# Row maxima on one core: 17 loads become 16, GpSimd's share grows from 36 to 53 squares, and most of its results return by small transfers

## The chip, the cores and the metric

The kernel runs on one core of a Trainium2 chip. The metric is the device time of one execution in microseconds (us). The time before is the median of three runs.

## What is computed

```python
def setup_inputs():
    batch, seq, dim = 32, 512, 1024
    return {"x": np.random.randn(batch, seq, dim).astype(np.float32)}

def reference(x):
    return np.max(x, axis=-1).astype(np.float32)
```

So 16384 rows of 1024 numbers come in (67.11 MB in float32), and one maximum for each row goes out (64 KB).

## The kernel before

**Units.** A *block* is 128 rows, one on each of the 128 partitions: 1024 numbers a partition, 0.524 MB. There are 128 blocks. A *square* is an eighth of a block, 128 rows by 128 columns.

**Loads.** `BLOCKS` lists how many blocks each load brings, in two groups; three blocks more, the last ones, come cut into six *pieces* (`PIECES`: which of the three blocks, and how many columns). All of it goes through one ring of 47 blocks in SBUF (`ring`), issued from SyncE's queue (loads L270, pieces L275). A load is issued as soon as the part of the ring that it fills has been read by all who need it. Transfers take eight semaphores in turn, and one that reuses a semaphore waits on its queue until the transfer that had it last has landed.

**VectorE's part.** `direct(j)` (d steps) reduces whole blocks of load j into the result columns, `partial(j)` (p steps) those squares of a shared block that GpSimd does not take, f steps the six pieces; all of it is the one reduction in `maximum`, L76. `merge` (m steps) joins the partial maxima of VectorE and GpSimd; m99 does it for the late loads together and is the last reduction of the kernel.

**GpSimd's part.** `SHARED` says for load j: of how many blocks (m) GpSimd takes how many squares each (parts), how many blocks go together in one chunk (per); the shared blocks are the load's last ones, and the fourth number is not used. Each chunk k runs through five steps:
- t (`turn`, L155): TensorE transposes each square into PSUM (`ps`), so that the 128 columns stand on the partitions.
- c (`fetch`, L166): ScalarE copies them to SBUF (`sb`, two buffers).
- r (`across`, L173): GpSimd's all-reduce takes the maximum over the partitions (`top`, two buffers); every partition then holds the row maxima, 128 for each square.
- b (`back`, L184): TensorE turns them back, one small matmul for each square, from partition 0 of `top` into `small` in PSUM.
- e (`keep`, L194): ScalarE copies them beside VectorE's partial maxima (`parts` or `joint`).

Before, chunks have two blocks of three squares or fewer, so at most 768 columns.

**Order.** `PLAN` is the order written out by hand; the number is the load for d, p and m, the chunk for t, c, r, b and e, and the piece for f. `in_turn` ties each instruction to the one before it on the same engine, so that the scheduler keeps the plan's order there. Loads and stores are not tied by it; they stand where the scheduler puts them.

**Stores.** Two stores go out from ScalarE's queue at the end: 116 columns (58 KB, L301), which wait for the first piece's reduction, and the last 12 columns (6 KB, L303), which wait for m99.

Of the kernel before, what the change touches and what calls it, by code (L numbers as in the profile page):

```python
# [8 lines left out]
F32 = mybir.dt.float32  # L9
# [1 line left out]


BLOCKS = [
    [2, 16, 14, 15, 13, 12, 10, 9, 8, 7, 6, 4],
    [3, 2, 2, 1, 1],
]
RING = 47

SHARED = {10: (6, 3, 2, 0), 12: (3, 3, 2, 0), 14: (2, 3, 1, 0), 16: (1, 3, 2, 0)}


RANK = {12: 1, 14: 2, 16: 2}


PIECES = [(2, 640), (0, 576), (1, 512), (1, 512), (0, 448), (2, 384)]


PLAN = """  # L30
    d0 d1 d2 d3 d4 d5 d6 d7 d8 d9 t0 p10 t1 c0 r0 t2 c1 d11 r1 c2 b0 e0 r2 b1 e1 t3 p12 t4
    c3 b2 c4 r3 d13 e2 r4 m10 t5 p14 b3 c5 t6 r5 d15 e3 b4 c6 t7 p16 e4 r6 b5 f0 c7 e5 f1 r7
    b6 f2 e6 f3 b7 f4 e7 f5 m99
""".split()

NOSYNC = mybir.DependencyInfo(mybir.DependencyClass.NoSync, mybir.DependencyReason.DATA)
# [4 lines left out]
def kernel(  # L41
# [5 lines left out]
    nc = tc.nc  # L47
    P = 128
    X = mybir.AxisListType.X
    ALU = mybir.AluOpType  # L50
# [7 lines left out]
    once = ctx.enter_context(tc.tile_pool(name="once", bufs=1))  # L58
    turned = ctx.enter_context(tc.tile_pool(name="turned", bufs=2))
    allr = ctx.enter_context(tc.tile_pool(name="allr", bufs=2))  # L60
    psum = ctx.enter_context(tc.tile_pool(name="psum", bufs=2, space=bass.MemoryType.PSUM))
    psmall = ctx.enter_context(tc.tile_pool(name="psmall", bufs=4, space=bass.MemoryType.PSUM))

# [5 lines left out]
    def in_turn(engine, inst):  # L69
        if engine in latest:  # L70
            tc.add_manual_dep(inst.ins, latest[engine].ins.name, NOSYNC, reason="in turn")
        latest[engine] = inst
        return inst

    def maximum(out, in_):
        return in_turn("DVE", nc.vector.reduce_max(out=out, in_=in_, axis=X))  # L76

    ident = once.tile([P, P], F32)
# [5 lines left out]
        out=colno, data0=ident, data1=ident, initial=-1.0, op0=ALU.add, op1=ALU.mult))  # L84
    in_turn("DVE", nc.vector.transpose(out=rowno, in_=colno[:, :32]))  # L85
    for q in range(1, P // 32):
        part = rowno[q * 32:(q + 1) * 32, 0:1]
        in_turn("DVE", nc.vector.tensor_scalar(  # L88
            out=part, in0=part, scalar1=float(q * 32), scalar2=None, op0=ALU.add))
    in_turn("DVE", nc.vector.tensor_scalar(  # L90
        out=ident, in0=colno, scalar1=rowno[:, 0:1], scalar2=None, op0=ALU.is_equal))

    loads = []
    views = []
    last = 1 + max(r for r, _ in PIECES)
    first = at = 0
    for sizes in BLOCKS:
# [5 lines left out]
        base = len(loads)  # L103
        b, place = 0, {}
        for i in sorted(range(len(sizes)), key=lambda i: RANK.get(base + i, 0)):
            place[i] = b
            b += sizes[i]
        for i, n in enumerate(sizes):
            if at + n > RING:
                at = 0  # L110
            b = place[i]
# [3 lines left out]
    assert first == I  # L115
    shared = [SHARED.get(j, (0, C, 1, 0)) for j in range(len(loads))]

    lead = [n - s[0] for (_, n, _, _), s in zip(loads, shared)]
    final = [j for j in range(len(loads)) if j in RANK]
    final.sort(key=lambda j: loads[j][3])  # L120
# [6 lines left out]
    chunks = []  # L127
# [3 lines left out]
    def rows(j):  # L131
        start, n, _, _ = loads[j]
        return ring[:, I + start * D:I + (start + n) * D].rearrange("p (i d) -> p i d", d=D)

    filled, turns, tops = {}, {}, {}
    fetched = {}
    smalls = {}

    def share(j):
        m, parts, _, _ = shared[j]  # L140
        if j in RANK:
            r = loads[j][3] + lead[j] - col0
            return joint[:, r:r + m, :]
        if j not in fetched:
            fetched[j] = once.tile([P, m, parts + (parts < C)], F32, name=f"parts{j}")
        return fetched[j]
# [30 lines left out]
    def back(k):  # L177
        j, r, q = chunks[k]
        parts = shared[j][1]
        small = psmall.tile([P, q, parts], F32)  # L180
        for i in range(q):
            for c in range(parts):
                w = (i * parts + c) * P
                in_turn("PE", nc.tensor.transpose(  # L184
                    out=small[:, i, c:c + 1],
                    in_=tops[k][0:1, w:w + P],
                    identity=ident[0:1, 0:1],
                ))

        smalls[k] = small  # L190

    def keep(k):
        j, r, q = chunks[k]
        in_turn("ACT", nc.scalar.copy(out=share(j)[:, r:r + q, :shared[j][1]], in_=smalls[k]))  # L194

    def select(k):
        j, _, q = chunks[k]
        B = q * shared[j][1]
        view = tops[k][:, :B * P].rearrange("p (b w) -> p b w", w=P)
        in_turn("POOL", nc.gpsimd.affine_select(  # L200
            out=view, in_=view, pattern=[[0, B], [-1, P]], compare_op=ALU.is_equal,
            fill=0.0, base=0, channel_multiplier=1))

    def sums(k):
        j, r, q = chunks[k]
        parts = shared[j][1]
        for i in range(q):
            for c in range(parts):
                w = (i * parts + c) * P
                in_turn("ACT", nc.scalar.activation(  # L210
                    out=tops[k][:, w:w + P], in_=tops[k][:, w:w + P],
                    func=mybir.ActivationFunctionType.Copy,
                    accum_out=share(j)[:, r + i, c:c + 1]))

    def direct(j):
        _, n, _, col = loads[j]
# [4 lines left out]
    def partial(j):  # L221
        m, parts = shared[j][:2]

        s = width - parts if j in RANK else 1
        maximum(share(j)[:, :, parts:], rows(j)[:, lead[j]:lead[j] + m, parts * P:].rearrange(
# [14 lines left out]
    before = [None] * last  # L240
    for r, w in PIECES:
        c, q = done[r], before[r]
# [33 lines left out]
            pieces.pop(0)  # L276

    gate = once.tile([P, 2], F32)
    steps = {"t": turn, "c": fetch, "r": across, "b": back, "e": keep, "s": select, "x": sums, "m": merge}
    for step in PLAN:  # L280
        issue()
        kind, k = step[0], int(step[1:])
# [50 lines left out]
```

## Time and profile before

| | us |
|---|---|
| median of three runs (163.75 to 163.92) | 163.78 |
| the profiled execution | 163.59 |
| its span, from the first to the last instruction | 161.81 |
| VectorE busy, 33 instructions | 135.5 (84%) |
| GpSimd busy, 13 instructions | 15.9 (10%) |
| TensorE matmul busy, 72 instructions | 13.3 (8%) |
| ScalarE busy, 17 instructions | 7.3 (5%) |
| input read, mean over the span | 67.11 MB, 415 GB/s |

Engines are named PE (TensorE), PEld (its weight loads), DVE (VectorE), ACT (ScalarE), POOL (GpSimd), SP (SyncE); a q behind the name means its queue, which issues transfers. L76 is line 76 of the kernel. The page divides the span into 40 slices of 4.05 us and gives the busy share in tenths. A timeline row is: start, duration, engine, line, operation, what it writes and reads, how many; in brackets the idle time of the engine before it and what ended that. A row on DMA issues gives KB and the time from issue to landing.

### The profile page before, as it was taken

To read this page: it belongs to the slowest core of one execution; us is meant where nothing else is said; L and a number is where in the kernel's file an instruction comes from. 1 tells how busy PE (TensorE), PEld (TensorE's weight loads), DVE (VectorE), ACT (ScalarE), POOL (GpSimd) and SP (SyncE) were. 2 spreads that over 40 slices of the span, in tenths; PEclk is the share of its full clock that TensorE was granted. 3 is DMA by queue.
4 is the path that set the end of the run, shared out by engine and by line. 5 is a ranking of instruction groups with operands and counts; after the bars stand their busy time and mean duration, and the time that the engine had idled before them with its cause. 6 is when DMAs were issued, how large, how long until landed. Compare 5 with 4: busy or idle time off the path is not lost.

```text
span 161.8 us, 304 instructions
## 1 busy us (share of the span) xinstructions
PE 13.3 (8%) x72; PEld 11.1 (7%) x72; DVE 135.5 (84%) x33; ACT 7.3 (5%) x17; POOL 15.9 (10%) x13
## 2 busy tenths in 40 slices
PE   0000000000000000000000000000000000647471
PEld 0000000000000000000000000000000000637350
DVE  3500009999999929999999999999999999999994
ACT  0020000000000000000000000000000000142230
POOL 0000000000000000000000000000000000097991
PEclk9999999999999999999999999999999999995555
DMA  5996998799999599999988997999999899999991
GB/s 198 579 486 292 518 472 383 312 454 454 486 486 486 243 454 421 421 448 561 401 389 389 486 466 344 437 437 421 478 429 439 376 475 395 433 410 412 408 389 38
DMA packets 3600, 67.18 MB, mean 415 GB/s; under 512 B 656, under 2 KB 912, under 8 KB 1680
## 3 DMA queue, kind: packets, MB, share of 16 engines
q1 hardware_dynamic: 3312, 67.11, 97.0%
q10 hardware_dynamic: 288, 0.07, 0.2%
HBM read 67.11 MB, written 0.07 MB: 415 GB/s over the span
## 4 chain that ended last, share of the span: by engine, by line
DVE 63%; DMA 35%; issue 0%; SPq 0%; DVEq 0%
DVE ring L76 58%; DMA ring<-in_x_dram 35%; DVE parts L76 3%; DVE joint L76 2%; SPq L270 0%; DVEq L328 0%; DVEq L76 0%
## 5 line engine op out<-in xcount | busy, mean ns | idle before, releaser
L76 DVE TENSOR_REDUCE ring<-ring 128x2 f32<-128x2048 f32 (+17 forms) x19 | 125.7, 6660 | 23.0 <-DMA ring<-in_x_dram 22.9
L173 POOL PARTITION_ALL_REDUCE top<-sb x8 | 15.6, 2013 | 134.9 <-ACT sb L166 134.5
L155 PE MATMUL ps<-ident,ring 128*128 128x128 f32 x36 | 8.9, 426 | 141.1 <-DMA ring<-in_x_dram 141.0
L155 PEld LDWEIGHTS ps<-ident,ring 128*128 128x128 f32 x36 | 7.0, 222 | 141.2 <-issue 141.2
L166 ACT COPY sb<-ps 128x768 f32<-128x768 f32 (+1 forms) x8 | 5.0, 640 | 139.1 <-PE ps L155 137.7
L184 PE MATMUL small<-ident,top 1*128 1x1 f32 x36 | 4.8, 238 | 4.4 <-POOL top L173 4.4
L184 PEld LDWEIGHTS small<-ident,top 1*128 1x128 f32 x36 | 4.1, 197 | 6.4 <-POOL top L173 5.0
L76 DVE TENSOR_REDUCE joint<-ring 128x3 f32<-128x1920 f32 (+2 forms) x3 | 4.4, 1483 | 0.0
L76 DVE TENSOR_REDUCE parts<-ring 128x6 f32<-128x3840 f32 x1 | 4.1, 4144 | 0.0
L166 ACT ACT_TABLE_LOAD x1 | 1.3, 1283 | 7.7 <-DVE ring L76 7.7
L194 ACT COPY joint<-small 128x3 f32<-128x3 f32 (+1 forms) x5 | 0.8, 164 | 2.3 <-PE small L184 2.3
L81 DVE MEMSET ident<- 128x128 f32 x1 | 0.2, 165 | 0.8 <-PEq L317 0.8
L288 POOL MEMSET gate<- 128x1 f32 x1 | 0.1, 100 | 7.3 <-DVE ring L76 7.3
L194 ACT COPY parts<-small 128x6 f32<-128x6 f32 x3 | 0.5, 166 | 2.6 <-PE small L184 2.5
L88 DVE TENSOR_SCALAR rowno<-rowno 32x1 f32<-32x1 f32 x3 | 0.4, 147 | 0.1
L83 DVE TENSOR_TENSOR_SCAN colno<-ident 128x128 f32<-128x128 f32 x1 | 0.4, 424 | 0.0
L90 DVE TENSOR_SCALAR ident<-colno,rowno 128x128 f32<-128x128 f32 x1 | 0.3, 286 | 0.0
L85 DVE STREAM_TRANSPOSE rowno<-colno 128x32 f32<-128x32 f32 x1 | 0.2, 211 | 0.0
L76 DVE TENSOR_REDUCE ring<-joint 128x6 f32<-128x24 f32 x1 | 0.2, 169 | 0.0
L76 DVE TENSOR_REDUCE ring<-parts 128x6 f32<-128x24 f32 x1 | 0.2, 168 | 0.0
L317 POOL MEMSET const-float32-0.0<- 128x1 f32 x1 | 0.1, 100 | 0.2 <-issue 0.2
L317 POOL MEMSET const-bfloat16-1.0<- 128x1 bf16 x1 | 0.1, 102 | 0.0
(3 smaller groups left out, 0.3 us busy)
## 6 DMA issues: line engine op xcount, KB each, us to landing
ring<-in_x_dram SPq DMA_DIRECT2D x1, 7680.0 KB, 57.6
ring<-in_x_dram SPq DMA_DIRECT2D x1, 7168.0 KB, 40.0
ring<-in_x_dram SPq DMA_DIRECT2D x1, 6656.0 KB, 33.6
ring<-in_x_dram SPq DMA_DIRECT2D x1, 6144.0 KB, 33.1
ring<-in_x_dram SPq DMA_DIRECT2D x1, 5120.0 KB, 26.2
ring<-in_x_dram SPq DMA_DIRECT2D x1, 4608.0 KB, 36.7
ring<-in_x_dram SPq DMA_DIRECT2D x1, 4096.0 KB, 32.9
ring<-in_x_dram SPq DMA_DIRECT2D x1, 3584.0 KB, 28.2
```

The lines of the kernel that those rows point to most:

```text
L76: return in_turn("DVE", nc.vector.reduce_max(out=out, in_=in_, axis=X))
L81: in_turn("DVE", nc.vector.memset(ident, 1.0))
L83: in_turn("DVE", nc.vector.tensor_tensor_scan(out=colno, data0=ident, data1=ident, initial=-1.0, op0=ALU.add, op1=ALU.mult))
L85: in_turn("DVE", nc.vector.transpose(out=rowno, in_=colno[:, :32]))
L88: in_turn("DVE", nc.vector.tensor_scalar(out=part, in0=part, scalar1=float(q * 32), scalar2=None, op0=ALU.add))
L90: in_turn("DVE", nc.vector.tensor_scalar(out=ident, in0=colno, scalar1=rowno[:, 0:1], scalar2=None, op0=ALU.is_equal))
L155: in_turn("PE", nc.tensor.transpose(out=ps[:, w:w + P], in_=rows(j)[:, lead[j] + r + i, c * P:(c + 1) * P], identity=ident,))
L166: in_turn("ACT", nc.scalar.copy(out=sb[:, :W], in_=filled[k][:, :W]))
L173: in_turn("POOL", nc.gpsimd.partition_all_reduce(top[:, :W], turns[k][:, :W], P, bass_isa.ReduceOp.max))
L184: in_turn("PE", nc.tensor.transpose(out=small[:, i, c:c + 1], in_=tops[k][0:1, w:w + P], identity=ident[0:1, 0:1],))
L194: in_turn("ACT", nc.scalar.copy(out=share(j)[:, r:r + q, :shared[j][1]], in_=smalls[k]))
L317: nc = _bacc.Bacc("TRN2", target_bir_lowering=False, num_devices=1)
```

## The change

Loads of 8 and 7 blocks go, and a second one of 15 comes in; the others keep their sizes. GpSimd now shares loads 8, 9, 10, 11, 13 and 15: all eight squares of two blocks of load 8 and of load 9 (one block a chunk, 1024 columns), one square of each of four blocks of load 10 (512 columns), and smaller chunks of three late loads (768, 384, 384, 384 and 256 columns). That makes ten chunks with 53 squares in place of eight with 36. Load 8 has 9 blocks, load 9 has 6.

For the first four chunks, 32 squares, a new step s (`spread`) comes between r and b: a transfer from ScalarE's queue takes the 1024 maxima from partition 0 of `top` to eight partitions of a new tile `lines` (two buffers), 128 on each, 4 KB in all; then `back` turns the eight squares in one matmul. The steps x and the old s, which the plan did not use, are deleted. The pieces keep their six sizes in another order, and the plan is new. The new transfer is not put through `in_turn`.

```diff
 BLOCKS = [
-    [2, 16, 14, 15, 13, 12, 10, 9, 8, 7, 6, 4],
+    [2, 16, 14, 15, 15, 13, 12, 10, 9, 6, 4],
     [3, 2, 2, 1, 1],
 ]
...
-SHARED = {10: (6, 3, 2, 0), 12: (3, 3, 2, 0), 14: (2, 3, 1, 0), 16: (1, 3, 2, 0)}
-RANK = {12: 1, 14: 2, 16: 2}
-PIECES = [(2, 640), (0, 576), (1, 512), (1, 512), (0, 448), (2, 384)]
+SHARED = {8: (2, 8, 1, 1), 9: (2, 8, 1, 1), 10: (4, 1, 8, 0), 11: (3, 3, 2, 0), 13: (2, 3, 1, 0), 15: (1, 2, 4, 0)}
+RANK = {11: 1, 13: 2, 15: 2}
+PIECES = [(0, 640), (1, 512), (2, 576), (1, 512), (2, 448), (0, 384)]
 PLAN = """
-    d0 d1 d2 d3 d4 d5 d6 d7 d8 d9 t0 p10 t1 c0 r0 t2 c1 d11 r1 c2 b0 e0 r2 b1 e1 t3 p12 t4
-    c3 b2 c4 r3 d13 e2 r4 m10 t5 p14 b3 c5 t6 r5 d15 e3 b4 c6 t7 p16 e4 r6 b5 f0 c7 e5 f1 r7
-    b6 f2 e6 f3 b7 f4 e7 f5 m99
+    d0 d1 d2 d3 d4 d5 d6 d7 t0 d8 t1 c0 r0 c1 r1 s0 t2 d9 b0 c2 t3 e0 r2 s1 c3 b1 t4 p10 e1
+    r3 s2 c4 b2 t5 e2 m8 p11 r4 s3 t6 c5 d12 b3 c6 b4 r5 e3 e4 m9 m10 p13 t7 t8 r6 c7 b5 d14
+    r7 e5 b6 c8 p15 t9 e6 f0 r8 c9 b7 f1 e7 f2 r9 b8 f3 e8 f4 b9 f5 e9 m99
 """.split()
...
+    spare = ctx.enter_context(tc.tile_pool(name="spare", bufs=2))
...
+    lines = {}
...
     def back(k):
         j, r, q = chunks[k]
         parts = shared[j][1]
         small = psmall.tile([P, q, parts], F32)
+        smalls[k] = small
+        if k in lines:
+            B = q * parts
+            in_turn("PE", nc.tensor.transpose(
+                out=small.rearrange("p i c -> p (i c)"), in_=lines[k][:B, :], identity=ident[:B, :B]))
+            return
...
+    def spread(k):
+        j, _, q = chunks[k]
+        B = q * shared[j][1]
+        lines[k] = spare.tile([P, P], F32, name="lines")
+        nc.scalar.dma_start(
+            out=lines[k][:B, :], in_=tops[k][0:1, :B * P].rearrange("o (b w) -> o b w", w=P))
...
-    steps = {"t": turn, "c": fetch, "r": across, "b": back, "e": keep, "s": select, "x": sums, "m": merge}
+    steps = {"t": turn, "c": fetch, "r": across, "b": back, "e": keep, "s": spread, "m": merge}
```

More of the change, by code (lines that the diff above doesn't have):

```diff
@@ L188, in back @@
                 ))
-        smalls[k] = small
     def keep(k):
@@ L194, in keep @@
         in_turn("ACT", nc.scalar.copy(out=share(j)[:, r:r + q, :shared[j][1]], in_=smalls[k]))
-    def select(k):
+    def spread(k):
         j, _, q = chunks[k]
         B = q * shared[j][1]
[L199 to L213, printed above, removed]
+        lines[k] = spare.tile([P, P], F32, name="lines")
+        nc.scalar.dma_start(
+            out=lines[k][:B, :], in_=tops[k][0:1, :B * P].rearrange("o (b w) -> o b w", w=P))
     def direct(j):
```

## The prediction

> **What bounds the kernel now.** I read the page's strips of 40 slices first, then busy time by stretches, then the timeline of the last 25 us engine by engine, with the DMA issues for when transfers landed. The profiled execution took 163.59 us: a span of 161.81 and 1.78 around it. It lies 0.19 under the median of 163.78; I sum against the profiled one and add the difference to the median.
>
> ```profile
> DVE 3500009999999929999999999999999999999994
> ...
> POOL 0000000000000000000000000000000000097991
> ...
> DMA  5996998799999599999988997999999899999991
> ```
>
> VectorE and the DMA are both full from slice 15 on; GpSimd works only at the end. Which one leads?
>
> ```profile
> 60.00:90.00 30.00, 0.00 (x0) 0.00 (x0) 29.84 (x2) 0.00 (x0) 0.00 (x0) 1.00 1.00 430
> 90.00:120.00 30.00, 0.00 (x0) 0.00 (x0) 29.97 (x3) 0.00 (x0) 0.00 (x0) 1.00 1.00 433
> 120.00:140.00 20.00, 1.19 (x6) 1.22 (x7) 20.00 (x4) 0.00 (x0) 0.00 (x0) 1.00 0.98 419
> ```
>
> The stretches show the two last columns, DMA share and GB/s: 430 to 433 GB/s at a share of 1.00, whatever VectorE does. The input is one stream that never pauses; its last piece was issued at 153.44 and took 5.3 us, so it landed at 158.7. VectorE ran level with it:
>
> ```profile
> 155.56 3.86 DVE L76 TENSOR_REDUCE ring<-ring 128x1 f32<-128x640 f32 x6
> 159.33 0.17 DVE L76 TENSOR_REDUCE ring<-joint 128x6 f32<-128x24 f32 x1
> ```
>
> Six pieces, each taken about when it lands; the last (0.54 us from 158.87) starts 0.15 after its landing. So work taken off VectorE shortens nothing beyond that 0.15; less work for it is hidden by the stream. What does have slack is GpSimd's path:
>
> ```profile
> 141.25 7.48 POOL L173 PARTITION_ALL_REDUCE top<-sb  x3 [133.47 <-ACT sb L166]
> 149.75 3.91 POOL L173 PARTITION_ALL_REDUCE top<-sb  x2 [1.02 <-ACT sb L166]
> 154.05 4.24 POOL L173 PARTITION_ALL_REDUCE top<-sb  x3 [0.39 <-PE small L184]
> ```
>
> The last result ends at 158.29; three transposes and ScalarE's copy follow, and the copy ends at 159.02:
>
> ```profile
> 158.85 0.16 ACT L194 COPY joint<-small 128x3 f32<-128x3 f32 x1 [1.25 <-PE small L184]
> 158.92 0.38 ACTq L301 DMA_DIRECT2D out_dram<-ring  x1
> 159.53 0.34 ACTq L303 DMA_DIRECT2D out_dram<-ring  x1
> ```
>
> The final merge (m99) started at 159.33, so this path had 0.3 us to spare. That is the number the change must not overrun.
>
> **One load fewer.** Same bytes, and 15 blocks stand where 8 and 7 stood. The 15-block load occupied the stream from 41.6 to 59.7 (18.1 us; issue plus time to landing), the 8 and 7 together from 113.0 to 131.2 (18.2). Gain: 0.07 us on every later landing. The pieces keep their sizes, and VectorE takes them in the new order: 0 for the stream, and for VectorE the same six durations. The ring keeps up: the 10-block load is issued when VectorE ends the second 15 blocks, at about 94, with the 13 in hand landed at 93.6 and the 12 streaming until 108.1. The 9-block load ends at block 106, where the 7-block load ended before, at 131.2; the 6-block load is where it was, 138.5.
>
> **VectorE** is relieved of 17 squares (about 0.13 us each, 2.3 us) and gets two merges more (0.09 each in step). All of that is hidden by the stream, except 0.07 to 0.15 us at the end.
>
> **GpSimd.** Three 768-wide reductions take 7.48 us (2.49 each), three 384-wide ones 4.24 (1.41 each). A line through the two: 0.33 + 2.81 ns a column, so 1024 wide is 3.21, 512 1.77, 256 1.05. It is an estimate; the bounds are 2.49 (no dearer than 768) and 3.32 (in proportion to it). I take the line, as 1024 is nearest to 768 and fixed cost is small. The new list is 4 x 3.21 + 1.77 + 2.49 + 3 x 1.41 + 1.05 = 22.4 us in place of 15.6. It starts earlier: t0 now reads the 9-block load. From the 6-block landing at 138.57 to the first copy took 1.79 us with six transposes; two more at 0.21 give 2.2, so c0 runs 133.4 to 134.4 (768 wide took 0.80, 384 0.48: 1024 is 1.01) and r0 starts at 134.45. Without a gap GpSimd would end at 156.9, well in time.
>
> **The gaps.** The built program's order decides here. Copies and reductions are held in the plan's order, but the new small transfers are not tied into it: on ScalarE's queue s1 stands directly behind s0, ahead of c2, and s3 behind s2, ahead of c4. A transfer waits for its reduction, and what is queued behind it waits too:
> - r0 134.45 to 137.66, r1 to 140.87. s1 waits for r1, then its issue holds the queue (0.38 for the store L301). c2 runs 141.35 to 142.36, r2 starts at 142.45. GpSimd stands still for 1.6 us.
> - r2 to 145.66, r3 to 148.87. s3 waits for r3; c4 (512 wide, 0.58) runs 149.35 to 149.93; r4 starts at 150.0. A second stop of 1.1 us.
> - r4 to 151.8, r5 to 154.3, r6 to 155.7, r7 to 157.1, r8 to 158.5, r9 ends at 159.63 (the last one's own end counts 0.1 over the step). Their copies are ready in time: c5 at 150.9, the others half a microsecond or more ahead.
> - After r9: before, 0.73 us from the last reduction's end to the copy's end, with three transposes; two now, 0.1 less. The copy ends at about 160.2, m99 starts at 160.27 in place of 159.33.
>
> **The end.** The first store now also stands behind that last copy, so it is issued at 160.2, and the second cannot be issued before 160.58, 1.05 later than the 159.53 above. Sum: +1.05 on the profiled 163.59 = 164.64; on the median 164.83. I say 164.8.
>
> VectorE meanwhile: m9 needs e3, which stands behind c6, which waits for r4 (151.8); VectorE gets there at 151.9 and goes on at 152.6, ending its last piece at 159.86. That costs nothing as long as m99 waits for GpSimd until 160.27; if that cover goes, 0.4 us of it remains. The single turn for eight squares spares TensorE 28 small matmuls (0.06 to 0.11 us each in step), all beside other work: 0.
>
> **The small transfers.** No transfer runs beside the stream in this trace on another queue. The nearest rows are the stores after it:
>
> ```profile
> out_dram<-ring ACTq DMA_DIRECT2D x1, 58.0 KB, 1.6
> ...
> out_dram<-ring ACTq DMA_DIRECT2D x1, 6.0 KB, 1.4
> ```
>
> Lower bound 1.4 us. Beside the stream a row in transit has to pass first: 24.6 KB rows at 433/16 = 27 GB/s for an engine is 0.9 us, the 8 KB rows later 0.3. One or two of them give 1.7 to 3.2; I take 2.3, nearest to the 6 KB store plus one row. In the schedule above s3 (issued at 148.95) holds one of the two buffers that r5 needs at 151.8, so up to 2.8 us is free; beyond that each microsecond costs one, and above 4.5 us more. Their 16 KB are under 0.1 us of the stream: below nothing is excluded, as nothing is taken from it. SP's queue is touched too: transfers share eight semaphores in turn, so the 1-block loads wait for s0 and s1, and pieces 1 and 3 for s2 and s3. Piece 3 would be issued at 151.5 for its turn at 156.9: covered by 5 us.
>
> The Trainium skill's page "DMA: Bandwidth & Descriptors" (Queues, rings and completion order) says that an engine drains a whole packet, typically 9 to 17 descriptors, of one queue before it turns to another. No run here shows it; by it a small transfer would wait for more than one row, which is the second rival below.
>
> **Rivals.**
> 1. *Not slower.* GpSimd's path comes out 0.95 us shorter than reckoned, so that stream and VectorE set the end again. That decides from 2.97 us for a 1024-wide reduction downwards (four of them, 0.24 each). For it: the lower bound of 2.49 and only two widths measured; the 768 rows with their fixed 0.33 speak against it. Then m99 starts at 159.25 and the time is 163.7, 0.1 below the median: "same".
> 2. *The small transfers are slow.* If one has to wait until the load in transit has landed (143.4 for s0 and s1, 149.6 for s2, 152.1 for s3, plus 0.5 of completion), t3 stands behind s0's turn on TensorE, r3 and s3 come late, r5 waits for s3, and the end moves by 2.7 us: 166.5. With 3 to 4 us each it is 165.1 to 166.1. For it: the stream is always full. Against: the page counts 3312 packets for 23 input transfers, 144 each, so that each of the 128 rows is a packet by itself:
>
> ```profile
> q1 hardware_dynamic: 3312, 67.11, 97.0%
> ```
> 3. *Faster by over 0.2%.* It needs 0.33 us. The stream gives 0.07 and VectorE's lag 0.15 at best; a quicker stream is not in sight at 433 GB/s in every stretch.
>
> **Numbers.** Chances: the forecast, 0.63; slow transfers, 0.22 (0.10 for 3 to 4 us, 0.12 for a whole load); not slower, 0.12; faster, 0.03. Forecast alone: 164.4 to 165.2 (0.2 either way on the reductions, 0.2 on the gaps). The range reaches up to rival 2's 166.5 and stops below at 164.1, leaving out rivals 1 and 3. A measurement of this kernel can tell about 0.2% (0.33 us) from no change: faster 0.03, same 0.12, slower 0.85.
>
> **What would show it.** Right: GpSimd's timeline with idle time of about 1.6 us before the third reduction and 1.1 before the fifth, both released by ScalarE's copy; 3.2 us a reduction; the last at 158.5; m99 waiting for ScalarE; input landed at 158.65. Wrong: c2 starting before r1 ends, 1024 wide under 3 us, a small transfer over 2.8 us, VectorE waiting for the stream at the end, or m99 following the last piece without a wait.

## The result, and the profile after

The change takes 168.72 us (168.61 to 168.78, five runs) against 163.83 (163.75 to 163.92) for the kernel before on the same chip: a ratio of 1.0296, 95% interval 1.0284 to 1.0307, or 4.9 us more. The profiled execution took 168.71 us, its span 166.94. The forecast was 164.8 with a range up to 166.5: the direction held, the size did not. In the trace of this run everything stands some 0.25 us later from the first load on (it lands at 5.58 here, 5.32 before; in the later runs between 5.47 and 5.70); differences below allow for it.

The strips of the page that answer to those shown of before:

```profile
DVE  3500009999999669995999999999999999994592
...
POOL 0000000000000000000000000000000077594791
...
DMA  5995999999959999969999889899899999999900
```

The input stream is nearly full in the first 38 of the 40 slices; the digits 4 and 5 on VectorE near the end and the 5 and 4 on GpSimd are new idle time. GpSimd's timeline from 130 us says whom it waited for (start, duration, what, how many; in brackets the idle time before and its releaser):

```profile
134.61 6.43 POOL L175 PARTITION_ALL_REDUCE top<-sb  x2 [126.56 <-ACT sb L168]
143.87 6.51 POOL L175 PARTITION_ALL_REDUCE top<-sb  x2 [2.82 <-DMA lines<-top]
152.39 1.78 POOL L175 PARTITION_ALL_REDUCE top<-sb  x1 [2.02 <-DMA lines<-top]
155.54 7.77 POOL L175 PARTITION_ALL_REDUCE top<-sb  x5 [1.37 <-DMA lines<-top]
```

Three stops, 6.2 us together, and each ends with the landing of a small transfer (`lines<-top`): the all-reduce needs the buffer of `top` that the transfer still reads. The reductions themselves take what was reckoned: 3.2 us for 1024 columns. ScalarE's timeline shows when the transfers were issued, and that its copies stand behind them:

```profile
137.87 3.84 ACTq L206 DMA_DIRECT2D lines<-top  x2
141.81 1.01 ACT L168 COPY sb<-ps 128x1024 f32<-128x1024 f32 x1 [5.91 <-POOL top L175]
...
147.12 3.91 ACTq L206 DMA_DIRECT2D lines<-top  x2
151.13 0.59 ACT L168 COPY sb<-ps 128x512 f32<-128x512 f32 x1 [3.96 <-POOL top L175]
```

TensorE's timeline shows where they landed, since the four turns of eight squares (L186) wait for nothing else:

```profile
143.72 0.27 PE L186 MATMUL small<-ident,lines 8*128 8x8 f32 x1 [2.90 <-DMA lines<-top]
...
146.70 0.27 PE L186 MATMUL small<-ident,lines 8*128 8x8 f32 x1 [0.81 <-DMA lines<-top]
...
152.25 0.27 PE L186 MATMUL small<-ident,lines 8*128 8x8 f32 x1 [4.24 <-DMA lines<-top]
...
155.41 0.27 PE L186 MATMUL small<-ident,lines 8*128 8x8 f32 x1 [0.77 <-DMA lines<-top]
```

The issues begin at 137.87, 141.07, 147.12 and 150.41; the semaphore increments in the trace complete at 143.68, 146.65, 152.21 and 155.36. So a transfer of 4 KB takes 5.8, 5.6, 5.1 and 5.0 us, where the forecast had 2.3 and at most 3.2. The waits reach VectorE too. Its merge m9 (the first row below) stands still for 3.76 us for e3, and so for s3's landing; it therefore comes to the six pieces only at 159.79. At the end m99 (the last row) waits 0.54 us for the last of GpSimd's squares:

```profile
155.91 0.17 DVE L77 TENSOR_REDUCE ring<-parts 128x2 f32<-128x16 f32 x1 [3.76 <-ACT parts L200]
...
159.79 3.65 DVE L77 TENSOR_REDUCE ring<-ring 128x1 f32<-128x640 f32 x6
163.97 0.18 DVE L77 TENSOR_REDUCE ring<-joint 128x6 f32<-128x24 f32 x1 [0.54 <-ACT joint L200]
```

So two paths end almost level, and both run through s3's landing: GpSimd's, and VectorE's by way of m9.

### The profile page after: what moved, and what is told of

Same layout as the page of the kernel before. It is cut to its first block, busy times and chain, and to the rows that moved or that the text cites. A ratio compares the mean times of both kernels' runs of the same rounds, so it can differ in the third digit from the quotient of the medians.

```text
span 166.9 us, 336 instructions
## 1 busy us (share of the span) xinstructions
PE 16.5 (10%) x78; PEld 13.5 (8%) x78; DVE 133.5 (80%) x34; ACT 10.1 (6%) x21; POOL 22.7 (14%) x15
## 4 chain that ended last, share of the span: by engine, by line
DMA 56%; DVE 28%; POOL 8%; issue 2%; PE 1%; POOLq 1%; ACT 1%; SPq 0%
DMA ring<-in_x_dram 50%; DVE ring L77 28%; POOL top L175 8%; DMA lines<-top 6%; PE ps L157 1%; POOLq L322 1%; ACT sb L168 1%; PE small L192 0%; SPq L264 0%; ACT joint L200 0%; POOLq L175 0%
## 5 line engine op out<-in xcount | busy, mean ns | idle before, releaser
L77 DVE TENSOR_REDUCE ring<-ring 128x2 f32<-128x2048 f32 (+15 forms) x18 | 123.4, 6902 | 25.2 <-DMA ring<-in_x_dram 25.2
L175 POOL PARTITION_ALL_REDUCE top<-sb x10 | 22.4, 2291 | 132.8 <-ACT sb L168 126.6
L157 PE MATMUL ps<-ident,ring 128*128 128x128 f32 x53 | 12.7, 419 | 135.6 <-DMA ring<-in_x_dram 135.6
L157 PEld LDWEIGHTS ps<-ident,ring 128*128 128x128 f32 x53 | 10.2, 220 | 135.8 <-issue 135.7
L168 ACT COPY sb<-ps 128x1024 f32<-128x1024 f32 (+4 forms) x10 | 7.1, 725 | 140.5 <-PE ps L157 127.8
L77 DVE TENSOR_REDUCE parts<-ring 128x4 f32<-128x3584 f32 x1 | 3.9, 3876 | 0.0
L192 PE MATMUL small<-ident,top 1*128 1x1 f32 x21 | 3.2, 246 | 3.0 <-POOL top L175 3.0
L192 PEld LDWEIGHTS small<-ident,top 1*128 1x128 f32 x21 | 2.7, 210 | 4.0 <-POOL top L175 4.0
L186 PE MATMUL small<-ident,lines 8*128 8x8 f32 x4 | 1.1, 270 | 8.7 <-DMA lines<-top 8.7
L186 PEld LDWEIGHTS small<-ident,lines 8*128 8x128 f32 x4 | 0.7, 178 | 10.3 <-DMA lines<-top 10.3
L200 ACT COPY parts<-small 128x8 f32<-128x8 f32 (+1 forms) x5 | 0.8, 165 | 2.8 <-PE small L186 2.5
```

The costliest lines, as they stand in the source:

```text
L157: in_turn("PE", nc.tensor.transpose(out=ps[:, w:w + P], in_=rows(j)[:, lead[j] + r + i, c * P:(c + 1) * P], identity=ident,))
L168: in_turn("ACT", nc.scalar.copy(out=sb[:, :W], in_=filled[k][:, :W]))
L175: in_turn("POOL", nc.gpsimd.partition_all_reduce(top[:, :W], turns[k][:, :W], P, bass_isa.ReduceOp.max))
L186: in_turn("PE", nc.tensor.transpose(out=small.rearrange("p i c -> p (i c)"), in_=lines[k][:B, :], identity=ident[:B, :B]))
L192: in_turn("PE", nc.tensor.transpose(out=small[:, i, c:c + 1], in_=tops[k][0:1, w:w + P], identity=ident[0:1, 0:1],))
```

## The experiments

Theory A: a small transfer beside the full stream takes 5 us or more, because rows of the input already stand ahead of it on every DMA engine, and the waits behind it are the loss. Rival B: the order on ScalarE's queue (s1 ahead of c2, s3 ahead of c4) is the loss. Rival C: GpSimd's and ScalarE's larger share is too much by itself.

### No transfers at all, and a surprise in it

```diff
-PLAN: ... r0 c1 r1 s0 t2 ... r2 s1 c3 ... r3 s2 c4 ... r4 s3 t6 ...
+PLAN: the same without s0, s1, s2, s3   (`back` then turns square by square)
```

> The changed kernel without the four small transfers: every square is turned back by a matmul of its own straight from the all-reduce's result, as before. If the small transfers are the whole loss (5 to 6 us each beside the stream, in place of the 2.3 forecast), GpSimd runs its 22.4 us from 134.5 without a stop, the stream sets the end again and the time is 163.7 (163.5 to 163.9). If GpSimd's larger share were too much by itself, it stays above 164.5. If ScalarE's larger copies were the cause, above 164.5 too.

Measured: 165.05 us (164.95 to 165.22), ratio 1.0075 (1.0061 to 1.0089). Neither number. GpSimd has no long stop left, and its last result reaches the merge by 159.35, so C does not hold; but VectorE waits 1.19 us for the input, which it did not before:

```profile
155.77 1.40 DVE L75 TENSOR_REDUCE ring<-ring 128x1 f32<-128x640 f32 x2
158.36 2.39 DVE L75 TENSOR_REDUCE ring<-ring 128x1 f32<-128x576 f32 x4 [1.19 <-DMA ring<-in_x_dram]
```

Its third piece landed at 158.33. Fifteen of the sixteen DMA engines had reported it by 157.10; one was 1.2 us late and stayed so, though all sixteen had reported the two pieces before it on time. The page's list of queues has a line that before lacks:

```profile
q1 hardware_dynamic: 3168, 67.11, 96.2%
q10 hardware_dynamic: 288, 0.07, 0.2%
q8 instruction: 1, 0.02, 0.0%
```

One packet of 16 KB, of the kind instruction: it ran from 156.12 for 1.09 us. With a matmul for each of those squares, TensorE has 106 matmuls in place of the change's 78. Two more kernels ask whether that is the 1.2 us. The first adds matmuls that nobody reads to the kernel before:

```diff
+            if step == "d6":
+                more = psum.tile([P, D], F32, name="ps")
+                for n in range(34):
+                    inst = in_turn("PE", nc.tensor.transpose(out=more[:, :P], in_=ident, identity=ident))
```

> The kernel before with 34 more transposes on TensorE, of the identity into PSUM, run behind the 10-block reduction (113.7 us) while TensorE has nothing to do; nobody reads them. TensorE then has 106 matmuls as in e1_turned_singly in place of 72. If e1's lost 1.2 us came from its longer instruction stream (one 16 KB instruction packet on a DMA engine that the input needs), the packet shows here too, one engine falls 1.1 to 1.2 us behind, and the time is 164.9 to 165.1. If e1 lost it by its new loads, pieces or plan, nothing changes: 163.8.

Measured: 163.96 us median, 163.77 to 165.20, ratio 1.0009 (0.9992 to 1.0026). The packet is there, but in the profiled execution it came at 158.64, as the last row of the input ended (158.63), and cost nothing there; so this run leaves open what a packet does within the stream. One of its ten executions took 165.20, 1.2 us more than the median; there is no trace of that one. The second takes eight matmuls away from e1:

```diff
-SHARED = {8: (2, 8, 1, 1), 9: (2, 8, 1, 1), 10: (4, 1, 8, 0), 11: (3, 3, 2, 0), ...}
+SHARED = {8: (2, 8, 1, 1), 9: (2, 8, 1, 1), 11: (3, 3, 2, 0), ...}   (p10 becomes d10; t4 to m10 go)
```

> e1_turned_singly without load 10 in GpSimd's share (VectorE reduces its four blocks whole): 49 squares, 98 matmuls on TensorE in place of 106, the same loads, pieces and order otherwise. If e1's 1.2 us came from the instruction packet that was fetched at 156.1, in the last two microseconds of the stream, the packet now comes after the stream's end or not at all, and the time is 163.7 to 164.1 (VectorE has 0.4 us more to do). If the loads, the pieces' order or the plan were the cause, it is 165 to 165.5.

Measured: 164.06 us (163.69 to 164.25), ratio 1.0007 (0.9997 to 1.0017). Its list of queues has no instruction packet, and VectorE's timeline no wait within the six pieces:

```profile
q1 hardware_dynamic: 3168, 67.11, 96.8%
q10 hardware_dynamic: 288, 0.07, 0.2%
```

```profile
156.02 3.64 DVE L75 TENSOR_REDUCE ring<-ring 128x1 f32<-128x640 f32 x6
```

Same loads, same order of pieces, same plan otherwise. So e1's 1.2 us go with the packet, which came 2.3 us before the end of the last row in e9: one engine alone was late, and by about the packet's 1.09 us. The trace does not name the engine that a packet ran on, so that it was this one is inferred. And a kernel with 49 squares on GpSimd and no small transfer costs what the kernel before costs. It also gains nothing, though VectorE has 13 squares less: the stream sets the end.

### The order on ScalarE's queue

```diff
-        nc.scalar.dma_start(
-            out=lines[k]...
+        in_turn("ACT", nc.scalar.dma_start(
+            out=lines[k]...))
```

> The changed kernel with the four transfers tied into the plan's order on ScalarE's queue, so that s1 stands behind c2 and e0 and s3 behind c4 and e2. If the order on the queue is what costs (s1 ahead of c2, s3 ahead of c4), the time falls to 164 to 165. If it is the time of each transfer, s1 now waits for e0, which waits for s0's landing, and so on: four transfers of 5.0 to 5.8 us in a row, and the time rises to 173 to 175.

Measured: 170.96 us (one run), 2.2 more than the change. So the built order is not what made the change slow: in the plan's own order s1 stands behind e0 and so behind s0's landing, the transfers run one after the other (5.8, 5.2, 5.1 and 2.5 us), and GpSimd waits three times for a landing, 2.8, 2.3 and 2.3 us. What the built order costs when the transfers are quick is seen in e7 below. The time is less than the 173 to 175 expected because the last transfer took 2.5 us (issued at 155.11, landed at 157.64). The pieces share semaphores with the transfers and were issued late, so the stream had run thin: by the trace's packets only 16 KB of rows an engine ended between the end of its issue and its first data, 1.1 us.

### What a transfer waits for

The probe puts seven such transfers into the kernel before, each behind a reduction and some dummy copies, at points where rows of different length stream in; the eighth comes after the stream.

```diff
+    probes = {"d1": 5, "d2": 0, "d3": 1, "d4": 4, "d5": 2, "d6": 5, "d7": 3, "f5": 0}
+    # after step X: so many copies of 1.0 us on ScalarE, then
+    nc.scalar.dma_start(out=caught[:8, :], in_=source[0:1, :1024] as 8 rows of 128)
```

> The kernel before, with seven transfers of the same form (4 KB from one partition to eight, ScalarE's queue) issued at about 48.4, 56.9, 77.0, 94.1, 105.1, 119.0 and 126.5 us, while loads with rows of 60, 60, 48, 40, 36, 32 and 28 KB stream in, and one of three partitions after the stream; nobody waits for them, so that the time should stay within 0.5 us of before. A wait of fixed length (some 75 KB ahead of it on each engine): 4.5 to 6.5 us each, whatever the row and wherever in the load. A wait until the load in transit has landed: 11.8, 3.3, 13.5, 8.5, 8.4, 4.2 and 5.3 us. A wait for a fixed number of rows (five): 13, 13, 10.5, 9, 8.3, 7.6 and 6.8 us. After the stream 1.4 to 1.6.

Measured, from the trace's packets and semaphore increments (us):

| issue begins, ends | rows in the stream | first data | all landed | from begin |
|---|---|---|---|---|
| 48.77, 50.01 | 60 KB | 54.57 | 57.64 | 8.9 |
| 57.19, 57.82 | 60, then 52 KB | 61.12 | 65.91 | 8.7 |
| 77.30, 77.92 | 48 KB | 82.13 | 84.93 | 7.6 |
| 94.36, 94.99 | 40 KB | 98.53 | 102.62 | 8.3 |
| 105.49, 106.12 | 36 KB | 109.78 | 112.26 | 6.8 |
| 119.37, 119.99 | 32 KB | 123.34 | 126.59 | 7.2 |
| 126.93, 127.56 | 28 KB | 130.84 | 132.19 | 5.3 |
| 160.55, 161.28 | none | 161.92 | 162.76 | 2.2 |

From the end of the issue to the first data it is 3.3 to 3.7 us in five of the seven, and 4.6 and 4.2 in the first and the third, beside rows of 60 and 48 KB; in the change it was 3.2 to 3.6 with rows of 4 to 16 KB. That is neither a number of rows nor the rest of the load, and nearly a fixed time. Counted in the trace's packets, 83 to 93 KB of rows an engine ended in that time in the last four of the seven, 70 to 128 KB in the three beside the longest rows, and 87 to 96 KB ahead of the change's four. That these rows had been handed to the engine before the transfer is inferred from the counts; the trace does not show what stands in an engine. The closing writes then come up to one row later still (2.3 us after the data with rows of 60 KB, at once with 28 KB). The first theory of the three was right in kind. Its upper bound of 6.5 us was 0.3 to 2.4 short for all but the last, and what it left out is that last row. The kernel as a whole took 165.85 us and not the expected 164.4 at most: its last merge started at 160.06 (159.33 before), and the last output store then stood behind the eighth probe on ScalarE's queue and was issued at 161.38.

The Trainium skill's page "DMA: Bandwidth & Descriptors" (Queues, rings and completion order) has an engine drain a whole packet of one queue, typically 9 to 17 descriptors, before it turns to the next. These runs do not show that for rows of this size: about five rows passed on each engine ahead of s0, eleven ahead of s2, two ahead of the first probe, and after them a single row between the data and its closing write.

The opposite case takes the rows away: a load waits until the first transfer has landed.

```diff
+            if issued == 10 and 0 not in lines:
+                return
             load = nc.sync.dma_start(out=rows(issued), in_=src)
+            if issued == 10:
+                tc.add_manual_dep(load.ins, first[0].ins.name, SYNC, reason="behind the transfer")
```

> The changed kernel with the 4-block load held back until the first small transfer has landed, so that the DMA engines have nothing ahead of it but the end of the 6-block load; the other three transfers go beside the stream as before. If the 5.8 us are rows that already stand ahead of it on each engine, the first takes 1.5 to 2.5 us, the second is back at 4.5 or more. If they are a cost of this form of transfer (one partition to eight), the first takes 5 us or more too. The time rises to 167 to 170, by the pause of the stream.

Measured: 169.21 us (one run), and the load that waits was issued at 139.80 (SyncE's timeline):

```profile
139.80 7.41 SPq L268 DMA_DIRECT2D ring<-in_x_dram  x6
```

The first transfer, issued at 137.93, landed at 139.75: 1.8 us in place of 5.8, its data 0.16 us after the end of the issue. The other three took 5.7, 4.9 and 5.6. The form and the queue are the same; only the rows ahead of it are gone. So the wait goes with the rows that stream in, as theory A has it. This run also shows the built order by itself. s1 still stands ahead of c2, s0 is no longer in the way, and GpSimd stands still before its third reduction for ScalarE's copies, 1.94 us where the prediction had 1.6:

```profile
143.04 3.22 POOL L176 PARTITION_ALL_REDUCE top<-sb  x1 [1.94 <-ACT parts L201]
```

So rival B's price is real, but in the change the landings cover it.

### Another queue

```diff
-        nc.scalar.dma_start(
+        nc.gpsimd.dma_start(
```

> The changed kernel with the four transfers issued from GpSimd's queue in place of ScalarE's; ScalarE's copies no longer stand behind them, GpSimd's reductions do. If the wait is in the 16 DMA engines, which all queues share, a transfer still takes 4.5 us or more and the time stays at 167 or more. If it is a matter of ScalarE's queue, the transfers take 1.5 to 3 us and the time falls to 164 to 165.5.

Measured: 172.15 us (one run). The four take 5.6, 5.8, 4.9 and 4.8 us from GpSimd's queue. So it is not ScalarE's queue. The kernel is slower than the change, since on GpSimd's own queue s0 stands behind r1: it is issued at 141.04 in place of 137.87, and r2 waits for its landing:

```profile
141.04 1.19 POOL L206 DMA_DIRECT2D lines<-top  x2
146.78 3.22 POOL L175 PARTITION_ALL_REDUCE top<-sb  x1 [4.55 <-DMA lines<-top]
```

### The same transfers with nobody behind them

```diff
-    [2, 16, 14, 15, 15, 13, 12, 10, 9, 6, 4],  RING = 47,  allr bufs=2
+    [2, 16, 14, 14, 15, 14, 12, 10, 9, 6, 4],  RING = 46,  allr bufs=3
+    the transfers put through in_turn, as in e2
+    PLAN: s1 right behind c2, s2 behind c3; b0 behind t4, e0 behind c4, m8 behind d12; b3, e3, m9 behind c8
```

> The changed kernel with the same four small transfers, but nobody standing behind them: three buffers of the all-reduce's results in place of two (the ring one block smaller, loads of 14, 14, 15, 14 in place of 14, 15, 15, 13), the turns back, copies and merges of those chunks two or more chunks later in the plan. If the price of a transfer is only the wait of those behind it, the transfers still take 5 to 6 us and the time falls to 163.8 to 164.2. If the transfers also slow the stream or GpSimd by themselves, it stays above 165.

Measured: 164.38 us (164.20 to 164.43), ratio 1.0030 (1.0020 to 1.0039). The transfers take 5.9, 5.5, 5.3 and 4.8 us as before, and 4.3 of the 4.9 us are gone. GpSimd waits for a transfer once, 0.23 us:

```profile
142.09 8.19 POOL L175 PARTITION_ALL_REDUCE top<-sb  x3 [0.96 <-ACT sb L168]
150.81 2.50 POOL L175 PARTITION_ALL_REDUCE top<-sb  x1 [0.53 <-ACT sb L168]
153.55 5.28 POOL L175 PARTITION_ALL_REDUCE top<-sb  x4 [0.23 <-DMA lines<-top]
```

It is 0.2 us above the expected band. Where the 0.5 us over the kernel before lies stays open. In the traces the last piece lands 0.42 later than before (159.14 against 158.72) and the last merge starts 0.46 later, but 0.33 of either is the later landing of the first load (5.65 against 5.32).

### Half of the transfers

```diff
-PLAN: s0 s1 s2 s3      e8: s0 s1 alone      e10: s2 s3 alone
```

> The changed kernel with small transfers for the two chunks of load 8 alone; the two of load 9 are turned back square by square from the all-reduce's result. If the price lies in the waits for buffers and turns behind each transfer, most of it was with the second pair, whose landing at 150 to 155 the reductions r4 and r5 and VectorE's merge waited for: 164.2 to 165.2 here. If each transfer costs alike, half of the loss remains: 166.2. TensorE has 92 matmuls, between the 78 of the change and the 106 of e1_turned_singly; an instruction packet as in e1 would add 1.2 us.

> The changed kernel with small transfers for the two chunks of load 9 alone; those of load 8 are turned back square by square. With 5.0 to 5.8 us for each transfer and the waits of the built order, r4, r5, e2, e3 and m9 stand behind them: 2.6 to 3.2 us above the kernel before, 166.5 to 167.1. If the first pair's 1.7 us (e8_first_pair) and this pair's add up to the whole 4.9, it is 167.0. If only the first transfer of a run of them were slow, 165 or less.

Measured, one run each: e8 165.56 us, span 163.8; e10 167.91 us, span 164.9. In both an instruction packet came after the last store had landed, in e10 3.0 us lie outside the span in place of some 1.8, so the spans are compared: with 162.1 for the kernel before on these chips, 1.7 and 2.8 us, together 4.5 of the change's 4.8. Each pair costs by its own waits, the second more. GpSimd's stops for a landing, one in e8 (first row) and two in e10:

```profile
143.88 8.27 POOL L175 PARTITION_ALL_REDUCE top<-sb  x3 [2.71 <-DMA lines<-top]
...
150.58 1.78 POOL L175 PARTITION_ALL_REDUCE top<-sb  x1 [2.15 <-DMA lines<-top]
153.78 7.76 POOL L175 PARTITION_ALL_REDUCE top<-sb  x5 [1.42 <-DMA lines<-top]
```

By its span e10 is where theory A had it (2.6 to 3.2 above the kernel before), by its time 0.8 above the expected band; e8 is 0.4 above its band.

## Why the prediction was wrong, point by point

- **What bounds it**: right. The stream sets the end wherever nobody waits for GpSimd (e9, e6), and 13 squares less on VectorE bought nothing.
- **One load fewer, the ring**: right. The second load of 15 blocks was issued, landed and reduced as reckoned (78.13; 0.2 for the late start), and the ring held nothing up.
- **GpSimd's durations**: right. Two 1024-wide reductions take 6.43 us (3.21 each), r5 to r9 7.77 (forecast 7.8); the sum is 22.4. Rival 1 had its ground there and falls.
- **The gaps from the queue's order**: right as a mechanism, c2 at 141.81 (141.35 forecast; issuing a transfer takes 0.64 us and not 0.38), and e7 shows a stop of 1.94 us where 1.6 was forecast. But as a price it was overtaken. GpSimd stood still where forecast, before the third and the fifth reduction, for 2.8 and 2.0 us, and not ScalarE's copies but the landings ended it. e2 shows that tying the transfers into the plan's order makes it worse: the built order starts each transfer as soon as its result is there.
- **The small transfers**: this is the term that failed. "One or two of them give 1.7 to 3.2; I take 2.3": measured 5.0 to 5.8. The bound took one or two rows in transit as all that can stand ahead; in the change five to nineteen rows of 16 to 4 KB, in e3 one to three long ones, passed on each engine in the 3.2 us or more before the first data, and in e7, with none, it was 0.16 us. No row of the trace before could show it, as nothing else ran beside the stream. With the measured times the same schedule gives the end: s0 lands at 143.7, so r2 and r3 run from 143.87 to 150.38; s3 then lands at 155.36; r5, which needs its buffer, starts at 155.54; r5 to r9 take 7.77; two turns, a copy, and the merge starts at 163.97, in place of 160.27.
- **"Beyond that each microsecond costs one, and above 4.5 us more"**: right, and it gives the size. r5 starts 3.7 us later than forecast (155.54 against 151.8). s0, at over 4.5 us, holds up r2, so that s3 is issued 1.46 later (150.41 against 148.95); and it holds its buffer for 5.13 us from there, 2.28 more than were free. The merge starts later by the same 3.7 (163.97 against 160.27), so the sum that gave 164.8 gives 168.5. The delays of the two pairs add up (e8, e10).
- **VectorE, "goes on at 152.6"**: the same term again. m9 went on at 155.91, as e3 stands behind s3's landing, and the last piece was done at about 163.4, half a microsecond ahead of the merge. The forecast's cover held, but only just: by this trace, relief for GpSimd alone would have gained about half a microsecond.
- **Piece 3, "covered by 5 us"**: the cover was used up. It was issued at 155.38, when s3 had landed, and the stream ran at 210 to 230 GB/s around 156.5 to 157. Its last piece landed at 159.46, half a microsecond late. That cost nothing, since m9's wait brought VectorE to the pieces only at 159.79.
- **Rival 2** had the right place and a wrong clock. Its landings (143.9, 143.9, 150.1, 152.6) followed the loads; the real ones did not, and came to 4.9 us and not 2.7.

## What to carry to other kernels

A small transfer beside a saturated load stream is priced by the stream, not by its bytes and not by a lone store after it: here 5 to 9 us against 1.8 with nothing ahead. Look for what waits for its landing before you price it. With two buffers, the buffer that it reads is needed again one step later: here a step of 3.2 us did not cover it, and with three buffers two steps all but did (e6). Look also for every engine that meets its result in order; here VectorE did, by its merge. Where that cannot be covered, a few more small instructions can be cheaper: turning each square by a matmul of its own cost nothing in e9, and in e1, with its instruction packet, 1.2 us. And where the input stream sets the end, moving work off the engine that runs level with it gains nothing.

## What was not expected of the hardware

- A longer instruction stream can delay the input. One 16 KB instruction packet took 1.09 us; shortly before the end of the stream one of the 16 DMA engines fell 1.2 us behind with it (e1 against e9), and when it came as the stream ended it cost nothing (e5). No run shows which length brings it when: with 106 matmuls on TensorE it came at 156.12 in e1 and at 158.64 in e5, with 92 only after the last store (e8, e10), with 98 not at all (e9).
- Issuing a small transfer from ScalarE's queue takes 0.63 us and 1.20 for the first one, against 0.34 to 0.39 for the change's and the earlier kernel's stores. The stream is not shown to be the reason: in e3 the eighth probe was issued after the stream and took 0.72, and the store behind it 0.74.
- GpSimd's all-reduce over 128 partitions costs 0.33 us + 2.81 ns a column, a line through 384 and 768 columns that also fits 512 and 1024 (1.78 and 3.21 us) and, with 256, the run of five (7.77).
